# Bias table's transfers on ScalarE's queue, the lambda terms one part earlier, memory tiles' work behind their transfers: a decoder layer on one core

## The chip, the cores and the metric

The kernel runs on one core of a Trainium2 chip. The metric is the device time of one execution in microseconds (us). Engines are named as in the profile: PE (matmuls), ACT (ScalarE), DVE (VectorE), POOL (GpSimd) and SP (SyncE, which only issues transfers here).

## The reference, cut to what matters

One decoder layer for 512 tokens of width 1024: a gated feed-forward network (FFN1), a mixer of a state-space part and eight heads of differential attention, attention into a fixed memory of 256 rows, and a second feed-forward network. Three pieces of it bear on the change:

```
def swiglu(h, w_in, w_out):
    gate, up = jnp.split(h @ w_in, 2, axis=-1)
    return (jax.nn.silu(gate) * up) @ w_out
...
        bias = jnp.transpose(rel_bias[rel_bucket(rel)], (2, 0, 1)).astype(jnp.float32)
...
        logits = logits + bias[None, :, None]
        logits = jnp.where(rel[None, None, None] <= 0, logits, -jnp.inf)
        p = jax.nn.softmax(logits, axis=-1)
        w = p[:, :, 0] - lam * p[:, :, 1]
...
        x = x + 0.5 * swiglu(rms_norm(x, norm_ffn1_w[l]), ffn1_w_in[l], ffn1_w_out[l])
```

The memory goes through `rms_norm` and is then multiplied into the keys and values of the cross attention; `lam` is made of exponentials of two sums over products of 64 parameters. Everything is float32.

## The kernel before, in words

Each float32 matmul is made of three faster ones: `split_into` (L152 to L161) makes a high part `wh` on ACT (L155, a copy to a rounded type) and a low part `wl` on DVE (L156, what is left), and PE multiplies high by high, low by high and high by low. A product therefore cannot start before ACT's copy, and its third matmul not before DVE's difference.

FFN1 goes in three parts of 8, 8 and 6 blocks of the hidden width. Each part has a first half, `ffn_quads`, and a second, `out_blocks` (L1198 to L1308, matmuls at L1225), which multiplies into the output with seven products of block sums in place of eight. In order they are: `oa` of "11" interleaved with `oe` of S1; `ob` of S2; `oa` of "12"; `ob` of S3; `oe` of S4; `ob` of "22". S1's weights are the sum B12 + B11, S3's B12 + B22. For these, `added` (L1248 to L1253) lets SP fetch B12 into a buffer `wr` (`fetch`, L1206) and POOL add the other block with an accumulating transfer (L1251). S2's sum is made by DVE (L1261). `wr` has six buffers, `wh` and `wl` three each. Behind "12", S3, S4 and "22" stands `update` (L1234 to L1238, DVE at L1236), which adds a result to `x`; in the third part it calls `square` (L550 to L552, ACT), whose sums of squares the mixer's norm needs. After the third part PE transposes `x` (`turn`, L1164 to L1172, tile `pxf`), and then makes the memory's keys (`memory_keys`, L1003, tile `pck`, weights `wck`).

The order of the work comes from three places. The class `Order` (L57 to L98) keeps a model time that the matmuls advance, runs the dense generators one behind the other, and steps generators spawned with a delay ("chains") once their time has come. SP and POOL issue in exactly the order in which the program is written by that (L104); POOL in particular issues transfers one after the other, and an instruction of it that waits holds all behind it. ACT, DVE and PE are put in order by the framework's scheduler.

`beside` (L543 to L546) is called ahead of each part's `out_blocks`. In the third it spawns two chains:

- `prepare` (L568 to L600): SP fetches `lamv`; DVE makes `lamp` and `lsum` (L575, L576), POOL `lexp` (L578), DVE `nlam` (L579, L580). SP fetches `rel_sb` and `hot` (L584, L587). DVE fills `rel_far`, POOL copies it to `rel_d` in memory (L591). PE multiplies `rel_sb` by `hot` into `prel` (L595), ACT copies it to `hot` (L597), POOL to `rel_d` (L598), and POOL lets `rel_d` be copied 128 times into `rel_z` (L600, 2.5 MB from memory to memory). The attention heads read `rel_z` later, as `bias`, by transfers that ACT issues (L703).
- `memory_in` (L979 to L992), 4 us later: SP fetches the memory in four transfers (L983), and each of eight tiles is squared (`nsq`, ACT at L385, the first `nacc` at L382), summed (`nacc`, DVE at L386) and split with its gain (`hm`, ACT at L159, DVE at L160).

Of the kernel before, what the change touches and what calls it, by code (L numbers as in the profile page):

```python
# [17 lines left out]
P = 128  # L18
T = 512
# [12 lines left out]
RW = 640  # L32
# [68 lines left out]
def body(tc, a, dbg=None):  # L101
    nc = tc.nc
# [12 lines left out]
    def nm(s):  # L115
        uid[0] += 1
        return f"{s}_{uid[0]}"

    def s2(s, dt=F32, shape=(P, T)):
        if math.prod(shape[1:]) <= T // 2:  # L120
            return sp.tile(list(shape), dt, tag="s1", name=nm(s), bufs=NHALF)
        return sp.tile(list(shape), dt, tag="s2", name=nm(s))
# [4 lines left out]
    def small(s, n, bufs=None):  # L127
        return tiny.tile([P, n], F32, tag=s, name=nm(s), bufs=bufs)
# [4 lines left out]
    def aux(s, shape=(P, T)):  # L133
        return aux_p.tile(list(shape), F32, tag="aux", name=nm(s))
# [6 lines left out]
    V, S, G = nc.vector, nc.scalar, nc.gpsimd  # L141
    od = Order()

    def mm(out, w, x, start, stop):
        od.t += (1 if w.dtype == R32 else 4) * (x.free_size() + 8) / 2400
        newest_mm[:] = [nc.tensor.matmul(out, w, x, start=start, stop=stop).ins]  # L146
# [16 lines left out]
    def split(s, src, scale=None, half=False, n=T):  # L163
        if half:
            both = s2(s, R32, (P, 2, T // 2))
            hi, lo = both[:, 0], both[:, 1]
        else:
            hi, lo = s2(s + "h", R32, (P, n)), s2(s + "l", R32, (P, n))
        last[:] = [i.ins for i in split_into(hi, lo, src, scale)]
        return hi, lo  # L170
# [12 lines left out]
    @contextmanager  # L183
    def behind(ins):
        with ExitStack() as after:
            for i in ins:
                after.enter_context(tc.issue_after(i))
            yield

    H = T // 2  # L190
# [350 lines left out]
    st_mix, h = Stat(), []  # L541

    def beside(ti):  # L543
        if ti == 2:
            od.spawn(prepare())
            od.spawn(memory_in(hm), 4.0)  # L546

    squares = small("squares", 8, bufs=1)

# [7 lines left out]

    od.spawn(st1.finish(), 18.0)
    od.add(ffn1(h1, wa_s, beside, square, fin1))


# [3 lines left out]
    rel_d = dram.tile([8, RW], F32, name="rel_d")  # L565
    rel_z = dram.tile([8, P, RW + 1], F32, name="rel_z")

    def prepare():  # L568
        lamv = cp.tile([P, 4, 64], F32, name="lamv")
        yield 0.0  # L570
        nc.sync.dma_start(lamv, a["lam"].partition_broadcast(P))
        lamp = small("lamp", 64, bufs=2)
        lsum = small("lsum", 2, bufs=1)
        for j in range(2):
            V.tensor_tensor(lamp, lamv[:, 2 * j, :], lamv[:, 2 * j + 1, :], ALU.mult)  # L575
            V.reduce_sum(lsum[:, j : j + 1], lamp, axis=AX.X)  # L576
        lexp = small("lexp", 2, bufs=1)
        G.tensor_tensor(lexp, euler[:, 0:1].to_broadcast([P, 2]), lsum, ALU.pow)  # L578
        V.tensor_tensor(nlam, lexp[:, 1:2], lexp[:, 0:1], ALU.subtract)  # L579
        V.tensor_scalar(nlam, nlam, -LAMBDA_INIT, None, ALU.add)  # L580
        V.tensor_scalar(wsub, par[:, C_SUBLN : C_SUBLN + 1], 1.0 - LAMBDA_INIT, None, ALU.mult)
        V.tensor_scalar(dskh, par[:, C_DSKIP : C_DSKIP + 8], 0.5, None, ALU.mult)
        rel_sb = small("rel_sb", 8, bufs=1)[:NUM_BUCKETS]
        nc.sync.dma_start(rel_sb, a["rel_bias"])  # L584
        hot = [s2("hot", shape=(NUM_BUCKETS, H)) for _ in range(2)]
        for i in range(2):
            nc.sync.dma_start(hot[i], a["hot"][:, i * H : (i + 1) * H])  # L587
        rel_far = small("rel_far", 64, bufs=1)[:8]
        V.memset(rel_far, MASKED)
        for c in range(T, RW, 64):  # L590
            nc.gpsimd.dma_start(rel_d[:, c : c + 64], rel_far)  # L591
        yield 7.5
        prel = aux("prel", (8, T))
        for i in range(2):
            mm(prel[:, i * H : (i + 1) * H], rel_sb, hot[i], True, True)  # L595
        for i in range(2):
            S.activation(hot[i][:8], prel[:, i * H : (i + 1) * H], AF.Copy, scale=-8.0)  # L597
            nc.gpsimd.dma_start(rel_d[:, i * H : (i + 1) * H], hot[i][:8])  # L598

        nc.gpsimd.dma_start(rel_z[:, :, :RW], rel_d[:, None, :].to_broadcast([8, P, RW]))  # L600

    def bc_c(t):
        return t[:, None, :].to_broadcast([P, 4, 16])
# [373 lines left out]
    def memory_in(dst):  # L979
        mem = []  # L980
        for k in range(0, KT, 2):
            mem.append(s2("mem2", shape=(P, 2, MEM)))
            nc.sync.dma_start(mem[-1], a["memT"][k : k + 2].rearrange("k p m -> p k m"))  # L983
        yield 4.0
        for k in range(KT):
            mk = mem[k // 2][:, k % 2]
            with behind(recent):
                st_mem.add(mk)
                dst.append(split("hm", mk, par[:, C_MEM + k : C_MEM + k + 1], True))
            yield 2.0  # L990
        yield 3.0
        yield from st_mem.finish(10.0)  # L992
# [78 lines left out]
    hm, hm2 = [], []  # L1071
# [393 lines left out]
```

## Time and profile before

| | |
|---|---|
| median of 3 runs (lowest to highest) | 1342.81 us (1341.29 to 1343.38) |
| profiled execution: its own time, its span | 1342.75 us, 1340.7 us |
| busy in the span: PE, DVE, ACT, POOL | 1297.0, 988.9, 708.3, 126.3 us |
| mean granted clock of PE | 0.988 |
| the third part's `out_blocks` | 314.61 to 373.10 us of the span |

A row of a timeline has start, busy time, engine, line, operation, out<-in, a count (xN for neighbours taken together), and in brackets the idle time before it on its engine with what ended it. A row of the waits has an engine and tile, what it waited for, and us in total, times, longest. A row of the chain has start, length and what it was; "issue" is time in which the engine waited for nothing that the profile shows. A row of the landings has the transfer, the queue that issued it, their number, KB each, and us from issue to landing.

### The profile page before, as it was taken

What the parts mean: (1) busy time and instruction counts of PE and PEld (TensorE: products, weight loads), DVE (VectorE), ACT (ScalarE), POOL (GpSimd) and SP (SyncE); (2) the same over time, 40 slices, a digit from 0 to 9 for tenths busy, and PEclk for the clock granted to TensorE, in tenths of its full rate; (3) what the DMA queues carried; (4) which work ended last, traced back from release to release, by engine and by line L of the source; (5) the groups of instructions that cost most, each with busy time, mean ns of one, the idle gap of its engine ahead of it and who ended that gap; (6) DMA issues with size and microseconds to landing.
All of it is one profiled execution on the core that took longest, in us unless ns stands there. A gap on an engine that the chain in (4) does not pass through costs nothing.

```text
span 1340.7 us, 20147 instructions
## 1 busy us (share of the span) xinstructions
PE 1297.0 (97%) x7728; PEld 1128.1 (84%) x7728; DVE 988.9 (74%) x1570; ACT 708.3 (53%) x1192; POOL 126.3 (9%) x148
## 2 busy tenths in 40 slices
PE   9999999997599999999999999999999999999996
PEld 7898998896397878787788877888889999989995
DVE  7978788788396477647867867645687877877886
ACT  6554555455374465535754556434465545555564
POOL 0001010010120101020110212120001100000001
PEclk9999999998799999999999999999999999999998
DMA  7557667874693624573366547776137876656662
GB/s 269 163 166 214 180 159 200 223 194 112 205 300 127 196 79 111 187 222 110 88 165 203 146 145 210 214 202 173 49 111 223 228 232 174 190 195 181 189 202 81
DMA packets 69503, 235.28 MB, mean 175 GB/s; under 512 B 8656, under 2 KB 10160, under 8 KB 69056
## 3 DMA queue, kind: packets, MB, share of 16 engines
q1 hardware_dynamic: 52912, 180.19, 39.2%
q0 software_dynamic: 14048, 47.27, 19.4%
q10 hardware_dynamic: 2448, 6.55, 1.4%
q8 instruction: 60, 0.98, 0.3%
q14 instruction: 35, 0.29, 0.1%
HBM read 231.82 MB, written 50.91 MB: 211 GB/s over the span
## 4 chain that ended last, share of the span: by engine, by line
PE 82%; issue 9%; DMA 4%; DVE 3%; ACT 1%; POOL 1%; POOLq 0%; SPq 0%; ACTq 0%; DVEq 0%
PE qb L240 10%; PE pm L146 9%; PE qe L240 7%; PE qa L240 7%; PE ob L1225 6%; PE pxbc L146 5%; PE oe L1225 3%; PE oa L1225 3%; PE pk L146 3%; PE pq L146 3%; PE pcq L146 3%; PE pv L146 3%; DMA wr<-in_f1b 3%; PE pz L146 2%; PE pck L146 2%
## 5 line engine op out<-in xcount | busy, mean ns | idle before, releaser
L155 ACT ACTIVATE wh<-wr 128x1024 fp32r<-128x1024 f32 (+1 forms) x329 | 334.7, 1019 | 382.1 <-issue 59.9
L156 DVE TENSOR_TENSOR wl<-wr,wh 128x1024 fp32r<-128x1024 f32 (+1 forms) x329 | 385.9, 1176 | 155.5 <-ACT wh L155 150.3
L146 PE MATMUL pxbc<-hnh,wh 128*128 128x512 f32 x128 | 52.2, 408 | 0.0
L146 PE MATMUL pxbc<-hnh,wl 128*128 128x512 f32 x128 | 50.3, 393 | 0.0
L146 PE MATMUL pxbc<-hnl,wh 128*128 128x512 f32 x128 | 50.2, 392 | 0.0
L734 ACT ACTIVATE ec<-ec,mn 128x512 f32<-128x512 f32 (+3 forms) x64 | 35.4, 555 | 24.2 <-DVE mn L733 24.2
L240 PE MATMUL qe<-s31h,wl 128*128 128x256 f32 x152 | 43.1, 283 | 0.0
L240 PE MATMUL qa<-h11h,wh 128*128 128x256 f32 x152 | 43.1, 283 | 0.0
L240 PE MATMUL qb<-s24h,wh 128*128 128x256 f32 x152 | 43.0, 283 | 0.0
L240 PE MATMUL qb<-s24l,wh 128*128 128x256 f32 x152 | 43.0, 283 | 0.0
L240 PE MATMUL qb<-s24h,wl 128*128 128x256 f32 x152 | 43.0, 283 | 0.0
L240 PE MATMUL qa<-hmh,wh 128*128 128x256 f32 x152 | 43.0, 283 | 0.0
L240 PE MATMUL qa<-hml,wh 128*128 128x256 f32 x152 | 43.0, 283 | 0.0
L240 PE MATMUL qb<-s31h,wl 128*128 128x256 f32 x152 | 43.0, 283 | 0.0
L240 PE MATMUL qe<-s24h,wh 128*128 128x256 f32 x152 | 43.0, 283 | 0.0
L240 PE MATMUL qe<-s24l,wh 128*128 128x256 f32 x152 | 43.0, 283 | 0.0
L240 PE MATMUL qe<-s24h,wl 128*128 128x256 f32 x152 | 43.0, 283 | 0.0
L240 PE MATMUL qb<-hmh,wh 128*128 128x256 f32 x152 | 43.0, 283 | 0.0
L240 PE MATMUL qb<-hml,wh 128*128 128x256 f32 x152 | 43.0, 283 | 0.0
L240 PE MATMUL qb<-hmh,wl 128*128 128x256 f32 x152 | 43.0, 283 | 0.0
L240 PE MATMUL qa<-hmh,wl 128*128 128x256 f32 x152 | 43.0, 283 | 0.0
L240 PE MATMUL qa<-h11h,wl 128*128 128x256 f32 x152 | 43.0, 283 | 0.0
(450 smaller groups left out, 4186.9 us busy)
## 6 DMA issues: line engine op xcount, KB each, us to landing
wr<-in_f2q SPq DMA_DIRECT2D x44, 512.0 KB, 4.4
wr<-in_f1q SPq DMA_DIRECT2D x40, 512.0 KB, 4.5
wr<-in_f1b SPq DMA_DIRECT2D x30, 512.0 KB, 5.0
isum<-in_f2q SPq DMA_DIRECT2D x22, 512.0 KB, 6.1
wr<-isum SPq DMA_DIRECT2D x22, 512.0 KB, 4.2
wsum<-in_f2b SPq DMA_DIRECT2D x20, 512.0 KB, 6.4
wr<-wsum SPq DMA_DIRECT2D x20, 512.0 KB, 4.5
wr<-in_f1q POOLq DMA_DIRECT2D x16, 512.0 KB, 6.5
```

The source lines that it names most:

```text
L146: newest_mm[:] = [nc.tensor.matmul(out, w, x, start=start, stop=stop).ins]
L155: S.activation(hi, src, AF.Copy),
L156: V.tensor_tensor(lo, src, hi.bitcast(F32), ALU.subtract),
L240: newest_mm[:] = [nc.tensor.matmul(out, a_[:, wc], b_, start=first and f == 0 and kp == 0 and j == 0, stop=kp == n - 1 and j == 2, skip_gr ...
L734: S.activation(ec[:, :n], ec[:, :n], AF.Exp, bias=mn, scale=-1.0, accum_out=sm[c][:, i : i + 1])
L1225: newest_mm[:] = [nc.tensor.matmul(ps, a_[:, ts], b_[:, ws], start=first and k == 0 and j == 0, stop=k == n - 1 and j == 2, skip_group_che ...
```

## The change

1. The lambda terms leave `prepare` and become a chain of their own, `lambdas`, spawned ahead of the first part's `out_blocks`, with pauses of 8, 4 and 4 us of model time.
2. The transfers of the bias table (`rel_far`, `hot`, `rel_z`) move from POOL's queue to ACT's, with pauses of 1.5, 2 and 6 us between the steps; the pause ahead of `prel` is 9 instead of 7.5 us.
3. `memory_in` starts 1 instead of 4 us behind the spawn, and pauses 9 instead of 4 us behind its transfers.

```diff
     def beside(ti):
-        if ti == 2:
+        if ti == 0:
+            od.spawn(lambdas())
+        elif ti == 2:
             od.spawn(prepare())
-            od.spawn(memory_in(hm), 4.0)
+            od.spawn(memory_in(hm), 1.0)
...
-    def prepare():
+    def lambdas():
         lamv = cp.tile([P, 4, 64], F32, name="lamv")
-        yield 0.0
         nc.sync.dma_start(lamv, a["lam"].partition_broadcast(P))
+        yield 8.0
...
+        yield 4.0
         lexp = small("lexp", 2, bufs=1)
         G.tensor_tensor(lexp, euler[:, 0:1].to_broadcast([P, 2]), lsum, ALU.pow)
+        yield 4.0
         V.tensor_tensor(nlam, lexp[:, 1:2], lexp[:, 0:1], ALU.subtract)
...
+    def prepare():
         rel_sb = small("rel_sb", 8, bufs=1)[:NUM_BUCKETS]
...
-        for c in range(T, RW, 64):
-            nc.gpsimd.dma_start(rel_d[:, c : c + 64], rel_far)
-        yield 7.5
+        yield 9.0
         prel = aux("prel", (8, T))
         for i in range(2):
             mm(prel[:, i * H : (i + 1) * H], rel_sb, hot[i], True, True)
+        for c in range(T, RW, 64):
+            S.dma_start(rel_d[:, c : c + 64], rel_far)
+        yield 1.5
         for i in range(2):
             S.activation(hot[i][:8], prel[:, i * H : (i + 1) * H], AF.Copy, scale=-8.0)
-            nc.gpsimd.dma_start(rel_d[:, i * H : (i + 1) * H], hot[i][:8])
-
-        nc.gpsimd.dma_start(rel_z[:, :, :RW], rel_d[:, None, :].to_broadcast([8, P, RW]))
+        yield 2.0
+        for i in range(2):
+            S.dma_start(rel_d[:, i * H : (i + 1) * H], hot[i][:8])
+        yield 6.0
+        S.dma_start(rel_z[:, :, :RW], rel_d[:, None, :].to_broadcast([8, P, RW]))
...
             nc.sync.dma_start(mem[-1], a["memT"][k : k + 2].rearrange("k p m -> p k m"))
-        yield 4.0
+        yield 9.0
```

Lines behind the change have numbers 7 higher (L1206 is L1213, L1225 is L1232, L1251 is L1258). Three places of the built order follow.

POOL in the third part, before (`wr_3446` and `wr_3485` are S1's two weights, `wr_3603` and `wr_3628` S3's):

```order
L578 TENSOR_TENSOR lexp_3421<-euler,lsum_3416 128x2
L591 DMA rel_d<-rel_far_3433 8x64 x2
L1251 DMA wr_3446<-in_f1b 128x1024
L1251 DMA wr_3485<-in_f1b 128x512
L598 DMA rel_d<-hot_3429 8x256
L598 DMA rel_d<-hot_3430 8x256
L600 DMA rel_z<-rel_d 1024x1x640
L1251 DMA wr_3603<-in_f1b 128x1024
L1251 DMA wr_3628<-in_f1b 128x512
```

and in the changed kernel (`wr_3452`, `wr_3483` are S1's, `wr_3602`, `wr_3627` S3's; `wr_3150` belongs to the first half of the part):

```order
L248 DMA wr_3150<-in_f1q 128x1024
L1258 DMA wr_3452<-in_f1b 128x1024
L1258 DMA wr_3483<-in_f1b 128x512
L1258 DMA wr_3602<-in_f1b 128x1024
L1258 DMA wr_3627<-in_f1b 128x512
```

The five transfers of the bias table and `lexp` are gone from between the accumulating ones; S3's stand right behind S1's.

ACT ahead of the part's S1 weights, before (`wh_3449` is the copy of S1's first weights):

```order
L155 ACTIVATE gh_3393<-th_3370 128x512
L382 ACTIVATE nacc_3520<-mem_594_3462 128x256
L159 ACTIVATE hm_3522<-mem_594_3462,par 128x256
L385 ACTIVATE nsq_3544<-mem_594_3462 128x256
L159 ACTIVATE hm_3547<-mem_594_3462,par 128x256
L385 ACTIVATE nsq_3574<-mem_595_3464 128x256
L385 ACTIVATE nsq_3613<-mem_595_3464 128x256
L385 ACTIVATE nsq_3638<-mem_596_3466 128x256
L155 ACTIVATE wh_3449<-wr_3446 128x1024
```

and in the changed kernel (`wh_3455` is that copy):

```order
L155 ACTIVATE gh_3407<-th_3384 128x512
L382 ACTIVATE nacc_3521<-mem_591_3438 128x256
L159 ACTIVATE hm_3523<-mem_591_3438,par 128x256
L385 ACTIVATE nsq_3559<-mem_591_3438 128x256
L385 ACTIVATE nsq_3585<-mem_592_3440 128x256
L385 ACTIVATE nsq_3618<-mem_592_3440 128x256
L385 ACTIVATE nsq_3656<-mem_593_3442 128x256
L385 ACTIVATE nsq_3680<-mem_593_3442 128x256
L385 ACTIVATE nsq_3708<-mem_594_3444 128x256
L385 ACTIVATE nsq_3754<-mem_594_3444 128x256
L155 ACTIVATE wh_3455<-wr_3452 128x1024
```

All seven further squares stand ahead of S1's copy now, and the second `hm` has moved behind it. DVE follows: ahead of its `wl` stood two `hm` and four sums, now one `hm` and seven sums.

ACT from S3's weights on, before (`wh_3606`, `wh_3631` are S3's copies, `wh_3655`, `wh_3679` S4's, `x_103` and `x_107` what S3 updates):

```order
L155 ACTIVATE wh_3606<-wr_3603 128x1024
L155 ACTIVATE wh_3631<-wr_3628 128x512
L155 ACTIVATE wh_3655<-wr_3653 128x1024
L155 ACTIVATE wh_3679<-wr_3677 128x512
L155 ACTIVATE wh_3695<-wr_3446 128x1024
L552 ACTIVATE junk_3648,squares_235<-x_103 128x512
L552 ACTIVATE junk_3651,squares_235<-x_107 128x512
```

and in the changed kernel (`wh_3605`, `wh_3630` are S3's copies, `wh_3649`, `wh_3673` S4's):

```order
L155 ACTIVATE wh_3605<-wr_3602 128x1024
L155 ACTIVATE wh_3630<-wr_3627 128x512
L609 DMA rel_z<-rel_d 1024x1x640
L554 ACTIVATE junk_3597,squares_235<-x_79 128x512
L554 ACTIVATE junk_3600,squares_235<-x_83 128x512
L159 ACTIVATE hm_3621<-mem_592_3440,par 128x256
L554 ACTIVATE junk_3642,squares_235<-x_103 128x512
L554 ACTIVATE junk_3645,squares_235<-x_107 128x512
L155 ACTIVATE wh_3649<-wr_3647 128x1024
L159 ACTIVATE hm_3659<-mem_593_3442,par 128x256
L155 ACTIVATE wh_3673<-wr_3671 128x512
```

S4's copies stood behind S3's and ahead of the squares of S3's result; now the squares stand ahead of them, and `rel_z` is issued behind S3's copies. On SP, the memory's four transfers stand ahead of B12's first fetch, and `lamv` in the first part, behind the first accumulated block's fetch.

## The prediction

> **What bounds the kernel now.** I read the page's first line of busy times, then the waits of TensorE (PE) around the third output part, then the chain of waits there.
>
> ```profile
> span 1340.7 us, 20147 instructions
> PE 1297.0 (97%) x7728; PEld 1128.1 (84%) x7728; DVE 988.9 (74%) x1570; ACT 708.3 (53%) x1192; POOL 126.3 (9%) x148
> PE ob L1225 <- ACT wh L155: 16.7, 1, 16.7
> PE oe L1225 <- ACT wh L155: 6.8, 1, 6.8
> ```
>
> PE is the bound: 1297.0 of 1340.7 us. What it does not work is 43.7 us, and two waits of the third output part make up 23.5 of them: 6.8 ahead of the first `oe` product (S1) and 16.7 ahead of the second `ob` product (S3). The names blame ScalarE's (ACT) copy `wh`; the chain, an excerpt of its pieces in order of time, shows who held that copy up.
>
> ```profile
> 309.03 25.54 issue
> 334.61 0.51 POOL rel_d L598
> ...
> 338.58 18.52 DMA wr<-in_f1b
> 357.19 1.07 ACT wh L155
> ```
>
> GpSimd (POOL), which issues in program order, stood 25.54 us before `rel_d`; then it issued `rel_z` (next fence), and only then the accumulating transfer that makes S3's weights. That transfer took 18.52 us, and PE waited for it. POOL's timeline and the transfers' landings (KB each, us from issue to landing) tell the same:
>
> ```profile
> 334.58 1.06 POOL L598 DMA_DIRECT2D rel_d<-hot  x2 [25.55 <-ACT hot L597]
> 337.48 1.11 POOL L600 DMA_DIRECT2D rel_z<-rel_d  x1 [1.84 <-DMA rel_d<-hot]
> 338.58 1.85 POOL L1251 DMA_DIRECT2D wr<-in_f1b  x2
> ...
> rel_z<-rel_d POOLq DMA_DIRECT2D x1, 2560.0 KB, 17.3
> wr<-in_f1b POOLq DMA_DIRECT2D x1, 512.0 KB, 18.5
> ```
>
> **Removed: the wait before S3.** The accumulate's own time, when nothing stands ahead of it in POOL's queue, is in the landings of 299 to 312 us; its raw weights, fetched by SyncE (SP), are the second row (312 to 332 us). SP asked for S3's first ones at 327.59.
>
> ```profile
> wr<-in_f1b POOLq DMA_DIRECT2D x1, 512.0 KB, 5.6
> ...
> wr<-in_f1b SPq DMA_DIRECT2D x2, 512.0 KB, 3.5
> ...
> 327.59 0.33 SPq L1206 DMA_DIRECT2D wr<-in_f1b  x1
> ...
> 336.86 1.28 ACT L1288 ACTIVATE u<-ob 128x512 f32<-128x512 f32 x2 [0.27 <-PE ob L1225]
> ...
> 326.35 1.22 DVE L1261 TENSOR_TENSOR wr<-wr,wr 128x1024 f32<-128x1024 f32 x1
> ...
> 341.19 0.39 PE L1225 MATMUL oa<-wl,gh 128*128 128x512 f32 x1
> ```
>
> The buffer of that fetch comes free behind VectorE's (DVE) sum at L1261, which stands later in the changed order (at worst some 1.5 us, to 329.1, for seven memory sums ahead of it, below). So: 329.1 + 3.5 (fetch) = 332.6, + 5.6 (accumulate) = 338.3, + 1.06 for ACT's copy. ACT comes to that copy behind `u` (x2, its waits on PE 0.9 later, see S1), one split and two `hm`, near 340.3, so it ends near 341.4. The product before S3 (`oa` of "12") issues its last matmul at 341.19; the next slot is 341.42, or 342.3 with the 0.9 that S1 loses below. The data is there 2 us before ACT is, and ACT 0.9 before PE, so I cost this wait at zero. How long PE takes from there is in the chain and in windows of four us (PE, PEld, DVE, ACT, POOL busy; PE's granted clock; DMA share; GB/s):
>
> ```profile
> 359.56 5.38 PE ob L1225 x16
> 364.93 4.08 PE oe L1225 x18
> 369.01 4.08 PE ob L1225 x18
> 373.10 3.49 PE pxf L150 x32
> ...
> 341.40:345.40 4.00, 0.18 (x1) 0.00 (x0) 1.85 (x4) 2.20 (x6) 0.00 (x0) 1.00 0.87 258
> 345.40:349.40 4.00, 0.00 (x0) 0.00 (x0) 0.00 (x0) 0.00 (x0) 0.00 (x0) 0.53 0.72 235
> 358.20:362.20 4.00, 3.87 (x8) 2.66 (x9) 3.05 (x3) 1.62 (x3) 0.00 (x0) 0.50 0.41 126
> 362.20:366.20 4.00, 4.00 (x18) 3.21 (x17) 2.16 (x4) 2.09 (x3) 0.00 (x0) 0.94 1.06 376
> ```
>
> An undisturbed product takes 4.08. S3, S4 and "22" need 12.24 from 341.42, to 353.66; now they end at 373.10. **Removed: 19.44 us**, of which 16.9 is idle and 2.6 is S3 itself, run at a granted clock of 0.50 after the idle (third window; the fourth's 0.94 adds 0.5 us of half clock, 4.5 in all, so 2.2 lost) and its late `wl`. The clock held 1.00 for the first 4 us of the idle (first window), and fell then.
>
> [...]
>
> **Longer: the wait before S1 (6.8).** Ahead of S1's split the built order puts seven squares of memory tiles on ACT and seven dependent sums on DVE; before there were four of each and a second `hm` split.
>
> ```profile
> 322.27 1.01 ACT L385 ACTIVATE nsq<-mem 128x256 f32<-128x256 f32 x3
> ...
> 322.83 1.48 DVE L386 TENSOR_TENSOR nacc<-nacc,nsq 128x256 f32<-128x256 f32 x3
> 324.27 1.83 DVE L156 TENSOR_TENSOR wl<-wr,wh 128x1024 fp32r<-128x1024 f32 x2
> ...
> 324.29 0.79 PE L1225 MATMUL oe<-wh,s31h 128*128 128x512 f32 x1 [6.77 <-ACT wh L155]
> ```
>
> ACT: three squares more (1.01 for three, with some 0.1 of the last one's drain) and one `hm` less (0.39) put `wh` 0.55 later. DVE: three sums more (1.48) and one `hm` less (0.4) put `wl` 1.1 later, and it is the third matmul that needs `wl`. The cost lies between 0.55 and 1.2; I take **+0.9**, nearer to DVE, since the matmul behind `wl` is the later one now as well.
>
> **New: a wait before S4.** Before, ACT split S4's weights (`wh_3655`) right behind S3's. Now `wh_3649` stands behind the squares of `x_103` and `x_107`, and these read what S3's result updates. The update and square behind "12" give the price:
>
> ```profile
> 340.94 1.43 DVE L1236 SCALAR_TENSOR_TENSOR x<-oa,col,x 128x512 f32<-128x512 f32 x2 [1.69 <-PE oa L1225]
> ...
> 341.72 0.63 ACT L552 ACTIVATE junk<-x 128x512 f32<-128x512 f32 x1 [3.19 <-DVE x L1236]
> 342.40 0.63 ACT L552 ACTIVATE junk<-x 128x512 f32<-128x512 f32 x1
> 343.03 0.89 ACT L159 ACTIVATE hm<-mem,par 128x256 fp32r<-128x256 f32 x2
> ```
>
> From the first update (340.94, that is 0.48 before the product's end) to the first instruction behind the squares (343.03) are 2.09 us. With E for the end of S3, `wh_3649` starts at E + 1.61 and ends 1.06 later, at E + 2.7, where S4's first two matmuls can go; `wl` takes 1.22 more, E + 3.9, and the third matmul, due at E + 0.45, waits for it. **+3.5.** Bounds: 2.4 (if DVE's and ACT's halves overlap more than behind "12"), 5.7 if the idle costs the clock as well (+2.2; a gap of 2.7 us lies under the 4 us held at 1.00), and 0 if the chip's ACT runs another order than the built one.
>
> **Behind "22"** the copies of `x` (`pxf`) and the `hm` splits that move there: between 0 and 1 us, as ACT has about 1 us of idle between its rows there; **+0.3**, near the lower end.
>
> **Costed at nothing.** (1) The ACT-issued transfers. Its eight `bias` issues show the price of one:
>
> ```profile
> L703 ACTq DMA_DIRECT2D bias<-rel_z x8: 326/327/477, 395.9 to 613.8; - x8
> ...
> DMA to landing us min/median/max: 2.5/4.1/8.0
> ...
> 335.95 0.63 ACT L155 ACTIVATE wh<-wr 128x512 fp32r<-128x512 f32 x1 [1.40 <-PE ob L1225]
> ```
>
> `rel_far` goes out at the kernel's start, where ACT waits for `x`; the two of `hot` stand ahead of `u`, behind 1.4 us of ACT idle; `rel_z` stands behind S3's splits, with some 3 us of free ACT before the squares of S3 (now its only covers: 0.33 to 3.4 us fit; beyond that the excess adds to the wait before S4). `rel_z` lands near 357 to 360 against a first reader near 381 (395.9 less the 14.7 below). (2) The lambda steps move to part one, where PE has no wait; `lexp` takes 0.73 us of POOL with over 10 us idle there. (3) Memory's four transfers ahead of B12's fetch on SP: S1's wait already ends on ACT and DVE, so 0 to 0.5.
>
> **The sum,** against the profiled execution's 1342.75 us: -19.44 + 0.9 + 3.5 + 0.3 = -14.7, so 1328.05. The median of the runs, 1342.81, lies 0.06 beside it: **1328.0**.
>
> **The rivals.**
>
> *S3's accumulate comes late all the same.* Its landing beside other traffic is longer elsewhere (page: ten at a median of 6.4; one POOL transfer between 280 and 400 us at 9.5), and `mem`, `hot` and S4's fetches are near it. Then 338.3 becomes 338.3 + (0.8 to 3.9), over the margin by 0 to 2; a longer gap and its clock loss make it +2 to +6: **1330 to 1334**. 0.15.
>
> *The wait before S4 is hidden:* DVE and ACT pass it before S3 ends, or it's short. Without the 3.5, or 2 of it: **1324 to 1326**. Against it stands that the squares cannot begin before S3's last matmul. 0.12.
>
> *The change doesn't do what it says:* all transfers share one capacity, and the accumulate still lands when `rel_z` does.
>
> ```profile
> 348.00:353.00 5.00, 0.00 (x0) 0.00 (x0) 0.00 (x0) 0.00 (x0) 0.00 (x0) 0.50 0.51 195
> ```
>
> Only POOL's issues (1.06 + 1.11 = 2.2) would be saved: **1340.6**. Against it: `rel_z` alone kept the transfer engines half busy (0.51), and in the new order the accumulates are asked for before `rel_z`, not behind it. 0.03. [...]
>
> *ACT is held while `rel_z` runs* (17.3, if its issue blocks): 14.2 beyond its 3 us of cover, and 2.2 of clock, end in S4's wait: **1344**, no change. No row of ACT's issues shows one over 0.48 us. 0.05.
>
> *Slower:* one mechanism ends there, `rel_z` slow in ACT's queue. In the built order SP's sixth fetch of `wck` waits for its landing; PE needs that weight some 15 us into `pck`, which decides once `rel_z` takes over 27.7 us from issue. A `bias` row of 256 KB landed in up to 8.0 us; ten of these, back to back, are 80 (upper end); the lower is 7.0 (2560 KB at the 376 GB/s of the window from 362.2). At 52 us, PE waits 24.3 and loses 2.2: **1354**. 0.05; the same transfer took 17.3 in POOL's queue.
>
> **Chances and range.** My forecast 0.60, late accumulate 0.15, S4 hidden 0.12, no gain from sharing 0.03, ACT held 0.05, slow `rel_z` 0.05. The range holds the forecast with its bounds (-1.1 to +2.2 on S4, 0.3 each on S1 and the rest), the late accumulate and the hidden wait: 1324.0 to 1334.5. About 0.2% (2.7 us) is what a measurement of this kernel can tell from no change; under 1340.1 counts as faster. Faster 0.88, same 0.06, slower 0.06.
>
> **What would show it.** POOL's row before S3's accumulate without the 25.55; that accumulate landing in 5 to 6.5 us; no `ob` wait of 16.7, but an `oe` wait of about 2.7 before S4, named for ACT's `wh`, and another near 7.5 before S1; the first `pxf` near 358.4; the granted clock at half in one stretch (321 to 329) instead of two. An accumulate still over 9 us, an ACT issue of `rel_z` over 3 us, or a `pck` wait on SP's fetch would prove it wrong.

## The result and the profile after

| | before | changed |
|---|---|---|
| median (lowest to highest) | 1342.49 us (1341.29 to 1343.38) | 1328.60 us (1327.39 to 1332.25) |
| profiled execution, span | 1342.75, 1340.7 us | 1328.03, 1326.2 us |

The ratio is 0.9902, 95% interval 0.988 to 0.9923, which leaves out 1: faster, by 13.9 us or 1.0%. The page's head of the changed kernel, and its PE waits between 250 and 480 us:

```profile
span 1326.2 us, 20148 instructions
...
PE 1296.8 (98%) x7728; PEld 1128.5 (85%) x7728; DVE 988.7 (75%) x1570; ACT 708.6 (53%) x1192; POOL 127.5 (10%) x143
```
```profile
PE oe L1232 <- ACT wh L155: 9.8, 2, 7.3
PE oe L1232 <- DVE wl L156: 1.4, 2, 0.9
```

PE's work is the same, only its idle time shrank. The `ob` wait of 16.7 is gone. The two `oe` waits on `wh` are 7.3 ahead of S1 and 2.5 ahead of S4. Why the first is gone stands in POOL's timeline, and in the landing of the transfers issued between 331 and 333 us:

```profile
307.54 0.85 POOL L1258 DMA_DIRECT2D wr<-in_f1b  x1 [6.85 <-DVE gl L156]
331.57 1.74 POOL L1258 DMA_DIRECT2D wr<-in_f1b  x2 [23.18 <-DVE wl L156]
```
```profile
wr<-in_f1b POOLq DMA_DIRECT2D x1, 512.0 KB, 5.7
```

POOL issues S3's accumulate at 331.57 instead of 338.58, and it lands in 5.7 us instead of 18.5. The chain through S3 and S4 shows what is late now:

```profile
337.36 4.08 PE oa L1232 x18
341.44 3.41 PE ob L1232 x15
344.88 0.76 DVE x L1243
345.67 0.72 ACT junk L554 x3
...
347.07 0.96 ACT wh L155
348.05 1.23 DVE wl L156
349.33 5.50 PE oe L1232 x16
354.83 4.08 PE ob L1232 x18
```

S3 follows "12" without a gap. Then the chain leaves PE: update of `x`, square, S4's `wh`, its `wl`. And S4 takes 5.50 for 16 matmuls where 18 take 4.08 elsewhere. The windows from S3's end on (behind POOL's count in brackets stand PE's granted clock, the share of the transfer engines and GB/s) show that this is the clock:

```profile
345.50:349.30 3.80, 0.76 (x3) 0.30 (x2) 2.46 (x5) 3.63 (x9) 0.00 (x0) 1.00 0.70 259
349.30:353.00 3.70, 3.67 (x9) 2.91 (x10) 2.50 (x4) 0.98 (x2) 0.00 (x0) 0.54 0.98 337
353.00:357.00 4.00, 4.00 (x19) 3.29 (x19) 3.06 (x4) 2.99 (x7) 0.00 (x0) 1.00 0.92 333
```

One more pair of rows matters for the experiments: ACT issues `rel_z` at 339.96, and SP, which has waited since 352.7, issues the sixth and seventh `wck` fetch at 366.18. The sixth waits for `rel_z` (SP's waits from 335 to 385 us name it, third fence), so `rel_z` landed 26.2 us after its issue, not 17.3. The reason is in the trace's semaphores: the transfers that SP and ACT issue use eight of them in turn as counters of completion (here 101, 103 to 105 and 107 to 110), and the sixth `wck` fetch, the eighth of these transfers behind `rel_z`, uses `rel_z`'s 103 again. SP waits for 103 ahead of it, and 103 rose for the last time at 366.12.

```profile
339.96 0.74 ACTq L609 DMA_DIRECT2D rel_z<-rel_d  x1
```
```profile
366.18 0.81 SPq L174 DMA_DIRECT2D wr<-in_wck  x2
```
```profile
SPq L174 <- DMA rel_z<-rel_d: 13.4, 1, 13.4
```

### The profile page after: what moved, and what is told of

It is laid out like the page before. It is cut to its first block, busy times and chain, and to the rows that moved or that the text cites. A ratio compares the mean times of both kernels' runs of the same rounds, so it can differ in the third digit from the quotient of the medians.

```text
span 1326.2 us, 20148 instructions
## 1 busy us (share of the span) xinstructions
PE 1296.8 (98%) x7728; PEld 1128.5 (85%) x7728; DVE 988.7 (75%) x1570; ACT 708.6 (53%) x1192; POOL 127.5 (10%) x143
## 3 DMA queue, kind: packets, MB, share of 16 engines
q1 hardware_dynamic: 52912, 180.19, 40.4%
q0 software_dynamic: 12880, 44.62, 18.9%
## 4 chain that ended last, share of the span: by engine, by line
PE 88%; issue 6%; DVE 3%; ACT 1%; POOL 1%; DMA 0%; POOLq 0%; SPq 0%; ACTq 0%; DVEq 0%
PE qb L240 12%; PE pm L146 9%; PE qe L240 8%; PE qa L240 8%; PE ob L1232 6%; PE pxbc L146 5%; PE oe L1232 4%; PE oa L1232 4%; PE pk L146 3%; PE pq L146 3%; PE pcq L146 3%; PE pv L146 3%; PE pz L146 2%; PE pck L146 2%; PE pa L146 2%
## 5 line engine op out<-in xcount | busy, mean ns | idle before, releaser
L240 PE MATMUL qb<-s31l,wh 128*128 128x256 f32 x152 | 43.0, 283 | 0.0
L240 PE MATMUL qb<-s31h,wh 128*128 128x256 f32 x152 | 43.0, 283 | 0.0
L240 PE MATMUL qa<-h11l,wh 128*128 128x256 f32 x152 | 43.0, 283 | 0.0
```

Of the source, the lines that this page charges most:

```text
L240: newest_mm[:] = [nc.tensor.matmul(out, a_[:, wc], b_, start=first and f == 0 and kp == 0 and j == 0, stop=kp == n - 1 and j == 2, skip_gr ...
```

## A ruler for the experiments

Single runs of one kernel scatter by 2 to 9 us, more than most questions here are worth. The place of the scatter can be seen: S1's wait starts (the last "11" matmul of the first interleaved round starts) between 314.5 and 319.6 us in the profiles of the fourteen kernels, and two kernels with the same code up to there, before and z_on_act, have 317.1 and 315.2. Behind that point the stretches repeat to some tenths, but for the first: kernels with the same S1 (changed, s4_ahead, s4_first, z_split) have 25.66 to 26.50 there, and both_first and z_split_both 21.52 and 22.91. So besides the medians I compare four stretches, by the starts of PE's rows: from that matmul to S3's first (S1 wait, S1, S2, "12", and any wait before S3; 24.3 without the latter), from there to the first of "22" (S3 and S4; 8.16 undisturbed), from there to `pck`'s first, and the keys, from there 193 matmuls on.

| kernel | median us | to S3 | S3, S4 | to pck | keys |
|---|---|---|---|---|---|
| before | 1342.49 | 41.17 | 10.56 | 7.49 | 23.40 |
| changed | 1328.60 | 26.11 | 13.39 | 7.80 | 23.42 |
| transfers_only | 1326.50 | 25.13 | 13.41 | 7.49 | 23.40 |
| memory_only | 1344.06 | 43.29 | 11.02 | 7.80 | 23.42 |
| s4_ahead | 1328.47 | 25.66 | 11.98 | 7.83 | 23.41 |
| mem_behind | 1326.56 | 22.29 | 13.46 | 7.81 | 23.43 |
| s4_first | 1331.65 | 26.48 | 8.55 | 8.31 | 30.98 |
| both_first | 1325.35 | 21.52 | 8.86 | 8.32 | 31.90 |
| pool_behind | 1349.66 | 24.21 | 8.16 | 8.76 | 44.35 |
| z_on_act | 1333.11 | 26.63 | 10.65 | 7.50 | 25.10 |
| z_split | 1332.49 | 26.50 | 8.55 | 7.80 | 28.82 |
| z_split_both | 1322.84 | 22.91 | 8.85 | 8.32 | 23.94 |

The ratios to the kernel before, with intervals: transfers_only 0.9892 (0.9879 to 0.9904), memory_only 1.0015 (1.0005 to 1.0025), s4_ahead 0.9907 (0.9889 to 0.9925), mem_behind 0.988 (0.9866 to 0.9895), s4_first 0.9917 (0.9903 to 0.993), both_first 0.9879 (0.986 to 0.9897), pool_behind 1.005 (1.0038 to 1.0062), z_on_act 0.9931 (0.9915 to 0.9947), z_split 0.9919 (0.9903 to 0.9934), z_split_both 0.9853 (0.9835 to 0.9871). x_beside and x_ahead, the last two kernels, ran once each and stand in no row.

## The experiments

**One part alone.** transfers_only takes from the change only the five transfers on ACT's queue and their pauses (the hunk in `prepare` without the lambda lines); memory_only takes only the two numbers of `memory_in`.

> Only the bias table's transfers go to ScalarE's queue, with the change's pauses; lambda and memory stand as before. Theory (the gain is POOL's queue set free): the wait of 16.7 before S3 goes, the wait before S4 comes as in the changed kernel (2.5 plus the clock), the wait before S1 stays at 6.8; about 1327, at or 1 to 2 us under the changed kernel. Rival (the gain needs the memory's earlier transfers too): S3 still waits, 1335 or more.

> Only the memory's start and pause are changed (1 instead of 4, 9 instead of 4); the bias table's transfers and lambda stand as before. Theory: seven squares and sums ahead of S1's weights lengthen the wait before S1 by 1 to 2 us, and the wait before S3 stays, since POOL is released by hot, which moves along; 1343.5 to 1344.5. Rival (memory's part brings some of the gain): 1340 or less.

Both went as the theory had it. The transfers alone bring 16.0 us. By the stretches that is 16.0 to S3, less 2.9 in S3 and S4, which is 13.2; of the rest, 2.6 lie ahead of S1 (314.53 against 317.13), in the scatter. The memory's numbers alone cost 1.5. The move of the lambda terms was not run alone. memory_only's PE waits show where its cost lies: S1 waits for `wh` 7.3 and then for `wl` 0.9, where the kernel before had 6.8 and nothing.

```profile
PE ob L1225 <- ACT wh L155: 16.7, 1, 16.7
PE oe L1225 <- ACT wh L155: 7.3, 1, 7.3
PE oe L1225 <- DVE wl L156: 0.9, 1, 0.9
```

**The new wait before S4.** s4_ahead makes S4's first split in the code ahead of S3's updates:

```diff
...
         yield from product(b_ps, sums[1], S3)
+        w4 = weights(blocks[B22], parts[0]) if finale is None else None
         for t in range(2):
             update(t + 2, 1, b_ps[t], -1)
         if finale is None:
-            yield from product(e_ps, blocks[B22], S4)
+            yield from product(e_ps, blocks[B22], S4, ahead=w4)
```

> The changed kernel with S4's first weights split ahead of the updates and squares of S3's result. Theory (the new wait before S4 is the order of ACT and DVE): the oe wait of 2.5 and its stretch at half clock go, 5.1 us less than the changed kernel, 1323.5. Rival (S4 waits for a buffer or a transfer anyway): within 1 us of the changed kernel, 1328.

Neither held: the median, 1328.47, is the rival's, but S4 waited for neither a buffer nor a transfer. ACT's half moved ahead, DVE's did not: its `wl` still started behind the updates, at 345.63. S3 and S4 took 11.98 instead of 13.39. The wait that is left is 1.9 us, and it costs the clock all the same:

```profile
344.80:347.90 3.10, 1.18 (x5) 0.86 (x5) 3.10 (x6) 3.10 (x8) 0.00 (x0) 1.00 0.76 281
347.90:351.30 3.40, 3.40 (x9) 2.62 (x8) 1.91 (x3) 1.07 (x2) 0.00 (x0) 0.50 0.92 358
351.30:355.00 3.70, 3.70 (x17) 3.02 (x16) 3.06 (x5) 2.69 (x6) 0.00 (x0) 0.99 1.04 412
```

s4_first also puts the updates behind both halves of that split (`latest` holds the two instructions of the last split):

```diff
...
-        for t in range(2):
-            update(t + 2, 1, b_ps[t], -1)
+        with behind(latest if finale is None else []):
+            for t in range(2):
+                update(t + 2, 1, b_ps[t], -1)
```

> The changed kernel with both halves of S4's first weights, ScalarE's and VectorE's, ahead of the updates and squares of S3's result. Theory (the wait before S4 is their order, on VectorE too): no oe wait between S3 and S4 and full clock in S4, so that the stretch from S3's end to S4's end takes 4.1 instead of 9.3 us; 1323.5. Rival (the updates, now 1.2 us later, hold the bank that 22 writes): a wait before 22 takes its place, 1326 to 1328.

The mechanism was as the theory said (8.55 instead of 13.39: 4.8 us gained), and yet nothing was gained: the median lies 3.1 us above the changed kernel's, and the intervals of the ratios overlap. The rival's place was wrong too: there is no wait before "22". The loss is in the keys, 30.98 instead of 23.42 in the profiled run, which was the longest of the six:

```profile
PE pck L146 <- DVE wl L156: 3.8, 1, 3.8
PE pck L146 <- ACT wh L155: 1.2, 1, 1.2
```
```profile
SPq L174 <- DMA rel_z<-rel_d: 16.3, 1, 16.3
```

The chain that ends there holds SP's sixth `wck` fetch at 369.49, 26.4 us after `rel_z`'s issue at 343.08, and SP had stood 16.3 us for `rel_z` (second fence). This is the mechanism of the prediction's slower rival, which I had given a chance of 0.05: the fetch waits for `rel_z`'s landing. Its condition, a landing after more than 27.7 us, was not met; PE came to the weight earlier.

**The memory's work behind the weights.** mem_behind ties each tile's work to the latest split of the output part:

```diff
...
-            with behind(recent):
+            with behind(latest):
```

> The changed kernel with each memory tile's square and split placed behind the latest split of the output part's weights. Theory (the wait before S1 is lengthened by the squares and sums ahead of its weights): that wait falls from 7.3 to about 4.5, and with less lost to the clock the time falls by 3 to 5 us, 1324 to 1325.5. Rival (the squares come back later ahead of S4 or the memory's keys): within 1 us of the changed kernel.

S1's wait fell to 4.4 and the stretch from 26.11 to 22.29, which is the 3 to 5 us of the theory; the median shows 2.0 of it.

```profile
PE oe L1232 <- ACT wh L155: 7.0, 2, 4.4
PE oe L1232 <- DVE wl L156: 0.5, 1, 0.5
```

both_first joins it with s4_first.

> The kernel of s4_first with the memory tiles' work behind the latest split as well. Theory (the two waits add): the wait before S1 falls to 4.4, none before S4; 4.2 + 5.1 less than the changed kernel, 1319.5. Rival (the memory's squares, pushed back, come in front of S4's weights or hold up the keys): 1323 or more.

S1 and S4 were each as short as expected (21.52 and 8.86), and the keys gave it back as in s4_first (31.90 in the profiled run, which was the longest of the six). The theory's 1319.5 was wrong, since it left the sixth fetch out; the rival had the time right (1325.35 is over 1323), its cause (the memory's squares) not.

**Splitting `rel_z`.** z_split is s4_first with this edit, z_split_both is both_first with it:

```diff
-        S.dma_start(rel_z[:, :, :RW], rel_d[:, None, :].to_broadcast([8, P, RW]))
+        S.dma_start(rel_z[:4, :, :RW], rel_d[:4, None, :].to_broadcast([4, P, RW]))
+        yield 60.0
+        with behind(list(recent)):
+            S.dma_start(rel_z[4:, :, :RW], rel_d[4:, None, :].to_broadcast([4, P, RW]))
```

> The kernel of s4_first with rel_z in two halves: heads 0 to 3 where rel_z stood, heads 4 to 7 some 60 us later. Theory (in s4_first the 5 us gained at S4 were given back at the sixth wck weight, whose fetch SyncE holds until rel_z has landed): the first half lands within 16 us of its issue instead of 26, SyncE's sixth fetch goes out at once, the pck waits of 3.8 and 1.2 go; 1323 to 1325 against 1331.7. Rival (the memory's keys starve for transfer bandwidth whatever SyncE waits for): pck waits of 3 or more stay, 1328 or more.

> The kernel of both_first with rel_z in the same two halves. Theory: it takes the 4.2 at S1 and the 5.1 at S4 and gives nothing back at the sixth wck weight, 1319 to 1321. Rival (bandwidth): pck waits of 3 or more stay, 1324 or more.

z_split failed: half the bytes still took 24.9 us, 1.5 less than the whole in s4_first. But its chain names the mechanism in full, from `rel_z` through SP's fetch to the keys (between fetch and `wl` stand ACT's `wh` and work on `x` that has its turn ahead of `wl` on DVE):

```profile
343.35 24.92 DMA rel_z<-rel_d
...
368.33 6.96 DMA wr<-in_wck
...
379.52 1.23 DVE wl L156
380.79 10.06 PE pck L146 x70
```

The rival's waits of 3 or more stayed, but not by its cause: the fetch itself is quick (6.96 against 7.3 and more in the changed kernel), so the memory's keys did not starve for bandwidth. Why half a table is no faster stands in windows in which `rel_z` was nearly alone: in z_split (first row) a share of 0.25 of the transfer engines and 95 GB/s, in s4_first (second fence) 0.51 and 193.

```profile
364.50:367.50 3.00, 3.00 (x27) 3.00 (x26) 2.15 (x4) 1.27 (x3) 1.91 (x2) 1.00 0.25 95
```
```profile
364.00:366.00 2.00, 2.00 (x18) 1.95 (x17) 0.66 (x3) 1.68 (x3) 0.17 (x1) 1.00 0.51 193
```

Eight heads kept half of the 16 engines busy, four a quarter. By these two shares that is one engine's time for each head (0.51 x 16 / 8 and 0.25 x 16 / 4 are both 1.0), an estimate: no view names the engine of a packet.

z_split_both was the fastest kernel of the study, 1322.84 us, 1.5% under the kernel before and 5.8 us under the changed one. That is 1.8 us over the theory's range; no `pck` wait of 3 us is left, so the rival did not come. Its sixth fetch went out at 363.25, 10.0 us before PE came to that weight (373.27), and the keys took 23.94. In the changed kernel that distance is 11.9; in s4_first it is 7.4, in both_first 8.5, in z_split 8.3, and all three wait. So here 10 us are enough and 8.5 are not. (The edge is not the same everywhere: x_beside, below, did not wait at that weight with 9.3, and z_on_act still had two waits of 0.7 and 0.5 with 10.6.) From `rel_z`'s issue to PE's coming, z_split_both and both_first have the same 34.5 us (338.82 to 373.27, and 339.74 to 374.2, when PE would have come without its wait); `rel_z` took 24.4 in the one and 26.0 in the other. So the 1.5 us that the split takes off the landing were the margin.

**Order or queue?** z_on_act is the kernel before with `rel_z` alone on ACT's queue, `hot` still on POOL's; pool_behind keeps everything on POOL's queue, but behind S3's accumulates.

```diff
-        nc.gpsimd.dma_start(rel_z[:, :, :RW], rel_d[:, None, :].to_broadcast([8, P, RW]))
+        S.dma_start(rel_z[:, :, :RW], rel_d[:, None, :].to_broadcast([8, P, RW]))
```
```diff
             S.activation(hot[i][:8], prel[:, i * H : (i + 1) * H], AF.Copy, scale=-8.0)
-            nc.gpsimd.dma_start(rel_d[:, i * H : (i + 1) * H], hot[i][:8])
+        yield 14.0
+        for i in range(2):
+            nc.gpsimd.dma_start(rel_d[:, i * H : (i + 1) * H], hot[i][:8])
```

> The kernel before with rel_z alone on ScalarE's queue; GpSimd still waits for hot ahead of S3's accumulates, which then overlap rel_z. Theory (most of the 18.5 was rel_z's data ahead in the same queue): the accumulate, issued near 336, lands in 6 to 8 us; the wait before S3 is 1 to 3, 1324 to 1327. Rival (all queues share the 16 engines and rel_z delays the accumulate from any queue): landing after 12 us or more, wait of 8 or more, 1333 or more.

> The kernel before, with hot and rel_z still issued by GpSimd, but behind S3's accumulating transfers instead of ahead of them; lambda and memory as before. Theory (GpSimd's order alone is the cause, not the queue that the table goes out on): the accumulate lands in 5 to 7 us, no wait before S3, and in this order S4's weights stand ahead of the squares, so none before S4; 1323, below the changed kernel. Rival (the table must leave GpSimd's queue, since rel_z disturbs the accumulates there): 1330 or more.

z_on_act: POOL still waits 25.7 us for `hot`, but the accumulate issued behind it at 333.48 lands in 7.0, and S3 waits 2.5:

```profile
332.31 1.05 POOL L598 DMA_DIRECT2D rel_d<-hot  x2 [25.68 <-ACT hot L597]
333.48 1.81 POOL L1251 DMA_DIRECT2D wr<-in_f1b  x2
```
```profile
wr<-in_f1b POOLq DMA_DIRECT2D x1, 512.0 KB, 7.0
```
```profile
PE ob L1225 <- ACT wh L155: 2.5, 1, 2.5
```

So POOL's wait for `hot` was worth 2 to 3 us of the 16.9, and `rel_z` ahead in the same queue, its issue (some 3 us of POOL) and its data, the rest. Here `rel_z` was issued 1.3 us behind the accumulate, so whether it would delay it from another queue when it goes ahead is left to x_beside. The time, 1333, was not the expected 1324 to 1327: 4.5 us more went in the keys and behind them (a fetch of SP stood 13.3 us for `rel_z` here too).

pool_behind: no wait before S3 or S4 (24.21 and 8.16, the best of all), as the theory said, and yet 7 us slower than the kernel before. The same `rel_z`, issued at 340.04 (339.96 in the changed kernel), on POOL's queue landed in 30.7, and five `wck` fetches issued from 340 to 349 landed in 3.8 to 17.8, a later one in 22.2, where three of the changed kernel's five had 7.3 to 9.7 (the trace does not give the other two). The rows are those of pool_behind, issues from 335 to 395:

```profile
wr<-in_wck SPq DMA_DIRECT2D x8, 512.0 KB, 16.7
...
rel_z<-rel_d POOLq DMA_DIRECT2D x1, 2560.0 KB, 30.7
```

The keys took 44.35, and 5 us more went behind them. Here no wait of SP names `rel_z` (in the traces of before and changed, POOL's transfers use eight semaphores of their own, 111 to 118), and SP issues its sixth to eighth fetch from 349.55 to 355.61. Whether POOL's packets (`rel_z`'s are of 5120 bytes in the trace of the kernel before; on ACT's queue, in the changed one, of 2560) or SP's flood crowded the weights out was not separated.

**Beside or ahead.** Two kernels add to the changed one a transfer of `rel_z`'s shape that nobody reads, on ACT's queue as S3's accumulate is issued, or on POOL's ahead of it.

```diff
-            S.activation(b_ps[t], a_ps[t], AF.Copy)
+            copied = S.activation(b_ps[t], a_ps[t], AF.Copy)
+        if here and each is not None:
+            with behind([copied.ins]):
+                S.dma_start(rel_y[:, :, :RW], blocks[B22][:8, None, :RW].to_broadcast([8, P, RW]))
```
```diff
+        if here and each is not None:
+            gate = small("lexp", 2, bufs=1)
+            G.tensor_tensor(gate, t_raw[parts[0]][:, :2], t_raw[parts[0]][:, :2], ALU.add)
+            G.dma_start(rel_y[:, :, :RW], blocks[B22][:8, None, :RW].to_broadcast([8, P, RW]))
         yield from product(b_ps, sums[1], S3)
```

> The changed kernel with one more transfer the size and shape of rel_z, from a weight block to a scratch tensor, on ScalarE's queue at the moment when GpSimd issues S3's accumulate; nobody reads it. Theory (in the kernel before, the accumulate was late because rel_z's packets stood ahead of it in GpSimd's own queue): the accumulate lands in 6 to 10 us beside it, wait before S3 at most 4. Rival (all queues share the 16 engines, and the queue does not matter): landing after 14 us or more, wait before S3 of 8 or more.

> The changed kernel with the same transfer on GpSimd's queue, about 2 us ahead of S3's accumulate; nobody reads it, and GpSimd waits for nothing that comes later than in the changed kernel but one sum of S2's weights. Theory: the accumulate lands with the end of that transfer, 13 us or more after its issue, and S3 waits 5 or more. Rival (GpSimd's late issue was the cause, not the data ahead): landing in 6 to 8, no wait.

x_beside (first fence): the accumulate landed in 10.3, a little over the theory's range and under the rival's 14; S3 started with no wait for it, although "12" ahead of it had itself lost 3.2 us in waits, which gave the accumulate that much more time. (PE then waited 9.3 for S3's last weights, whose copy stood behind ACT's `rel_z` issue at 354.85; that waited for `hot`'s transfers, behind the extra one, and ACT stood idle for 10.9. ACT's queue did to ACT what POOL's had done to POOL.) x_ahead (second fence): the gate sum came later than I had meant, so POOL issued the accumulate at 337.56 and not near 331; it landed 26.5 us later, just behind the extra transfer, and S3 waited 23.8.

```profile
wr<-in_f1b POOLq DMA_DIRECT2D x1, 512.0 KB, 10.3
```
```profile
rel_y<-in_f1b POOLq DMA_DIRECT2D x1, 2560.0 KB, 24.4
...
wr<-in_f1b POOLq DMA_DIRECT2D x1, 512.0 KB, 26.5
```

So the same 2.5 MB, issued 1 us ahead, cost an accumulate 4.6 us from another queue, and 20.8 from its own. The 4.6 us fit two transfers that share engines (from 333.5 to 345 us of x_beside POOL's queue took 45.6% of the 16 engines' time, ACT's 28.1% and SP's 13.0%), and the 20.8 show that the queue in which a small transfer stands decided whether it waited for the large one. (x_ahead had two such transfers under way, `rel_z` itself on ACT's queue, issued 1.1 us behind the accumulate, so 20.8 is an upper bound for one alone; the kernel before, with one, had 18.5 against 5.7, which is 12.8.) Each ran once: x_beside took 1340.5 us and x_ahead 1349.4. The changed kernel's page calls POOL's queue (q0, 44.62 MB) software_dynamic, SP's (q1, 180.19 MB) and ACT's (q10, 9.20 MB) hardware_dynamic. No run puts the table on SP's queue or another of POOL's, so what in POOL's queue holds the small transfer, the data or the handling of its packets, is open.

## Why the prediction was right, and where it was not

The forecast was 1328.0, the median 1328.6. Term by term, by the stretches:

| term | forecast | measured |
|---|---|---|
| wait before S3 and S3 slowed | -19.4 | -16.9 - 2.4 = -19.3 |
| wait before S1 | +0.9 | 26.11 - 24.29 = +1.8 |
| wait before S4 | +3.5 | 13.39 - 8.16 = +5.2 |
| behind "22" | +0.3 | +0.3 |
| keys | 0 | 0.0 |
| sum | -14.7 | -12.0 |

- **Removed.** Right in mechanism and size. The accumulate's 5.7 was the 5.6 taken from its neighbour, and ACT, not the data, came last, as worked out (data at 337.27, ACT's copy from 339.01). z_on_act, and x_beside against x_ahead, show that it was the queue.
- **S1.** Right in place, half the size, and outside the bounds of 0.55 to 1.2. Both halves add up, where I took one: `wh` 0.5 later, `wl` a further 0.8, and 0.45 more at half clock.
- **S4.** The wait came as worked out: S4's third matmul started 3.5 us late (349.33). The step that was off: "a gap of 2.7 us lies under the 4 us held at 1.00". The gap was 2.54, and the clock halved 4 us after S3's end, for 3.4 us, which cost the other 1.7. So the sign "at half in one stretch (321 to 329) instead of two" did not come: there were two, 318.8 to 329.0 and 349.5 to 352.9. In the long idle before, the clock had also held for 4 us, but that is how long the fall took, not how long a gap may be. My upper bound of 5.7 held. A gap of 1.92 in s4_ahead was enough to halve the clock, and one of 2.20 in z_on_act was not (last section).
- **Costed at nothing.** `rel_z` landed at 366.2, not 357 to 360: the 17.3 us were those of POOL's queue with PE idle, and it took 26.2. That cost nothing in the changed kernel, but of the slower rival's distance, 27.7 - 17.3 = 10.4 us, some 1.5 was left by its own scale. s4_first, where PE comes to the weight earlier, fell over that edge. (The 52 us from which that rival's 1354 was worked out have no source in the prediction.)
- **The sum.** The stretches give -12.0 and the profiled runs -14.7. Of the rest, 2.0 lie ahead of S1 (317.13 against 315.17): in the kernel before, ACT had in its profile a wait of 2.62 on a transfer in the second part that the other did not have, and the fourteen profiles scatter by more than that. So the agreement to 0.6 us is partly luck; two terms were 2.6 too small together, and the interval of the ratio, -16.1 to -10.3 us, holds both sums.

## What to carry to other kernels

POOL's queue, issued in program order, delayed S3's accumulate in two ways: by the issuer's wait for `hot` (25.55 us, worth 2 to 3 of the 16.9), and by the big transfer itself (the rest). The second was the larger, and putting the transfer in another engine's queue removed both. Moving it to the end of the same queue removed both as well, but that kernel became slower in what followed, for a reason that was not separated. Before costing a background transfer at nothing, look for who waits for its landing by a shared counter: s4_first gained 4.8 us in front of it and gave 7.6 back there (30.98 against 23.42 in the keys). And a PE gap of about 2 us cost here 1.7 us by half clock behind it (1.92 in s4_ahead, 2.54 in the changed kernel), or nothing (2.20 in z_on_act), by where it fell (below).

## What was not expected of the hardware

- In the profiles of the kernel before and the changed one the granted clock changed in steps of 3.41 us: its stretches at 0.50 between two at 1.00 lasted 6.83 and 17.07 us (before, from 321.74 and 345.63) and 10.24 and 3.41 us (changed, from 318.78 and 349.50), which are 2, 5, 3 and 1 of them. In these two profiles, from 9 us on, a step at 1.00 in which PE was busy 0.91 us or less was followed by one at 0.50, and none with 2.32 or more was; from 0.50 it came back behind steps with 3.37 us or more, and not behind 1.91 or less. So what a gap cost went by how much of one step it filled, and not by its length alone. With the gap of 2.54 in the changed kernel PE was busy 0.91 us of a step (first fence: PE's busy time stands behind the comma, the clock before the last two numbers), with the 1.92 in s4_ahead 1.49; each cost a step at half clock. In z_on_act a gap of 2.20 from 386.11 on was shared by two steps, in which PE was busy 2.14 and, with one more gap of 0.53, 1.95: the clock stayed at 1.00 (second fence).

```profile
346.09:349.50 3.41, 0.91 (x3) 0.47 (x4) 2.07 (x4) 3.41 (x9) 0.00 (x0) 1.00 0.66 262
349.50:352.91 3.41, 3.41 (x9) 2.64 (x10) 2.30 (x4) 0.78 (x1) 0.00 (x0) 0.50 1.01 346
```
```profile
383.96:387.37 3.41, 2.14 (x18) 1.94 (x17) 0.03 (x1) 0.89 (x3) 0.00 (x0) 1.00 1.03 422
387.37:390.78 3.41, 1.95 (x7) 1.34 (x8) 3.29 (x5) 1.44 (x3) 0.00 (x0) 1.00 0.98 401
390.78:394.19 3.41, 3.41 (x16) 2.81 (x16) 2.78 (x4) 3.02 (x4) 0.00 (x0) 1.00 0.95 378
```

- `rel_z` with four outer rows took nearly as long as with eight (24.9 us in z_split against 26.2 in the changed kernel and 26.4 in s4_first), at half the share of the engines (0.25 against 0.51).
- `rel_z` took 17.3 us on POOL's queue with PE idle, 26 on ACT's beside the key weights, and 30.7 on POOL's beside them.
